# The last eighth of a split down projection: column half by column half, its sums merged into an early reloaded residual

## The chip, the cores and the metric

One Trainium2 chip, one of its cores. The metric is the device time of one execution in microseconds (us). The kernel before takes 873.03 us (median of 3 runs, 872.73 to 873.03).

## The reference

Two request groups of 256 tokens (512 rows, model width 1024) go through one encoder layer. Three attention branches are gated, summed and projected, a residual is added, and then comes the part at issue:

```python
h2 = rms_norm(x, norm2_g)
x = x + jnp.square(jax.nn.relu(h2 @ w_up)) @ w_down     # 1024 -> 4096 -> 1024
...
return rms_norm(x, final_norm_g)                        # over the whole row of 1024
```

All of it is float32.

## The kernel before

A float32 product is made of three passes on TensorE: each operand is split into a high part (a copy by ScalarE, in a rounded type) and a low part (original minus high, by VectorE), and `mm3` (L193) issues high x high, high x low, low x high. Splitting a weight chunk of 128x1024 is one ScalarE and one VectorE instruction, which write `w` tiles; the chunk arrives from memory by a transfer on SP's queue into one of two `raw` buffers (`chunk`, L163). A third chunk's transfer waits until the low part of the first is made.

The work is a list of units (`unit`, `run`, L178). `run` fetches the chunks of the units to come, as many ahead as `ahead[0]` says (3 in this stretch), and calls the units in turn. VectorE, ScalarE and TensorE keep the order in which the code issues (`InOrder`); SP's and POOL's queues are ordered by the framework's scheduler. `later` holds closures (evacuations, sums) that `flush` runs behind the next unit's matmuls or ahead of them; `lows` holds low parts that `lower` issues.

The MLP runs in 8 rounds (`NC`, L1045). Round c makes 512 of the 4096 hidden columns (`up`, in halves of 12 products each, `put_up` squares them) and, interleaved with these, seven products of the down projection of round c-1, in a scheme with fewer products than the plain one (Winograd's): `form` makes sums of hidden tiles, `parts` makes weight sums in `blk` tiles (4 per round, 8 buffers, `load_blocks` L900), `product` multiplies, and `add_to` adds the result to eight accumulators `acc` of 128x512, named V, 11, 12, 21 and G, two token tiles each. So a round is 15 x 12 products.

The last round's own hidden columns have nothing to interleave with: their down projection is done plainly, from `LAST` (four split hidden tiles of 128x512, the fourth made last) and four weight chunks 11, 12, 21, 22. There are 4 token tiles t of 128 rows and 2 column halves hh of 512, each of these 8 pieces needs 12 products. Before, `last_down(t)` does both halves of one t, `combine(t)` (L998) adds V to the accumulators and the sums to the residual tile `xt[t]`, and `finish` (L1023) adds the piece from PSUM, squares it on ScalarE for the final norm, and multiplies by the final gain `gf`. `final` (L1029) makes 1/rms on VectorE and POOL, scales the two halves on ScalarE and VectorE and writes them out. The residual (unscaled, stored in memory as `x1d` in round 0) and `gf` are fetched by `fetch_x1` (L987) behind the last round:

```python
    unit(fetch_x1)
    kept = []
    unit(lambda *w: (kept.extend(w), last_down(0, *w)), *[(block(NC - 1, n),) for n in ("11", "12", "21", "22")])
    for t in range(1, NT):
        unit(lambda t=t: last_down(t, *kept))
```

Of the kernel before, what the change touches and what calls it, by code (L numbers as in the profile page):

```python
# [10 lines left out]
F32 = mybir.dt.float32  # L11
F32R = mybir.dt.float32r
AF = mybir.ActivationFunctionType
ALU = mybir.AluOpType
AX = mybir.AxisListType

P = 128
# [3 lines left out]
NT = T // P  # L21
# [56 lines left out]
def encoder_kernel(ctx: ExitStack, tc: tile.TileContext, a: dict, out: bass.AP):  # L78
    nc = tc.nc
    V, A, E = (InOrder(tc, e) for e in (nc.vector, nc.scalar, nc.tensor))  # L80
    G, SP = nc.gpsimd, nc.sync

    sb = ctx.enter_context(tc.tile_pool(name="sb", bufs=1))
# [8 lines left out]
    def nm(s):  # L92
        cnt[0] += 1
        return f"{s}{cnt[0]}"
# [4 lines left out]
    def h2(s="h", dt=F32):  # L99
        return sb.tile([P, T], dt, tag="h2", name=nm(s), bufs=20)  # L100

    def bank(s="ps"):
        return ps.tile([P, 512], F32, tag="ps", name=nm(s))
# [36 lines left out]
    p = bank("warm")  # L140
# [6 lines left out]
    def unit(fn, *srcs):  # L147
        units.append((fn, srcs))
# [20 lines left out]
    ahead = [1]  # L169
# [3 lines left out]
    def lower(keep=0):  # L173
        for fn in lows[:len(lows) - keep]:
            fn()
        del lows[:len(lows) - keep]
# [16 lines left out]
    def mm3(o, wh, wl, xh, xl, first, last, more=False):  # L193

        E.matmul(o, wh, xh, start=first, stop=False, skip_group_check=more)
        E.matmul(o, wh, xl, start=False, stop=False, skip_group_check=more)
        E.matmul(o, wl, xh, start=False, stop=last, skip_group_check=more)
# [73 lines left out]
    later = []  # L271
# [395 lines left out]
    def flush(n=2):  # L667
        for fn in later[:n]:
            fn()
        del later[:n]  # L670
# [164 lines left out]
    NC = 8  # L835
# [10 lines left out]
    def block_tile():  # L846
        return at[0].tile([P, 1024], F32, tag="blk", name=nm("blk"), bufs=8)

    def turn_x1(t, hh):

        b = bank("tp")
        for i in range(4):
            E.transpose(b[:, i * P:(i + 1) * P], X1[4 * hh + i][:, t * P:(t + 1) * P], ident)
        x = h2("xt")
        A.activation(x, b, AF.Copy)
        A.activation(h2("junk"), b, AF.Square, accum_out=ss[:, t, hh:hh + 1])
        A.dma_start(x1d[t, :, hh * 512:(hh + 1) * 512], x)
# [11 lines left out]
    def up(w, ff, half):  # L869

        if half == 0:
            up_bank[ff] = w, bank()
        w, p = up_bank[ff]
        for k in range(4 * half, 4 * half + 4):
            c = slice(k * P, (k + 1) * P)
            mm3(p, w[0][:, c], w[1][:, c], H[k][:, 0], H[k][:, 1], k == 0, k == KD - 1)
        flush(9)
        if half:
            later.append(lambda: put_up(ff, p))
# [14 lines left out]
    LAST = []  # L894

    def block(c, n):
        k, h = ((0, 0), (0, 1), (1, 0), (1, 1))[("11", "12", "21", "22").index(n)]
        return a["w_dn"][c // 2, h, 2 * (c % 2) + k]

    def load_blocks(c):  # L900

        if c in blocks:
            return
        t = {n: block_tile() for n in "T2BC"}
        for n, b in (("T", "11"), ("2", "21"), ("C", "12"), ("B", "22")):
            SP.dma_start(t[n], block(c, b))
        G.dma_start(t["C"], block(c, "22"), accum_op=ALU.add)
        blocks[c] = t
# [20 lines left out]
    def form(c, name):  # L929

        lo, hi = UP[c, 0], UP[c, 1]
        A11, A21, A12, A22 = lo[:, :, :S], lo[:, :, S:], hi[:, :, :S], hi[:, :, S:]

        def less(u, v):
            d = h2("f").rearrange("p (j t) -> p j t", j=2)
            V.tensor_tensor(d, u, v, op=ALU.subtract)
            return d

        if name in ("P1", "P2", "Q4"):
            src = {"P1": A11, "P2": A12, "Q4": A22}[name]  # L940
        elif name == "Q5":
            src = forms[c, "S1"] = less(A21, A22)
        elif name == "Q6":
            src = forms[c, "S2"] = less(A11, forms.pop((c, "S1")))
        elif name == "P7":
            src = less(A11, A21)
        else:
            src = less(A12, forms.pop((c, "S2")))
        x = s4("f")
        xh, xl = (x[:, i].rearrange("p (j t) -> p j t", j=2) for i in range(2))  # L950
        A.activation(xh, src, AF.Copy)
        lows.append(lambda: V.tensor_tensor(xl, src, f(xh), op=ALU.subtract))
        forms[c, name] = x

    acc, banks = {}, {}
# [26 lines left out]
        later.append(lambda: [add_to(to, i, ps_[i], ALU.add if sign > 0 else ALU.subtract) for i in range(2)])  # L982


    xt, gf = {}, []

    def fetch_x1():  # L987
        for t in range(NT):
            xt[t] = sb.tile([P, 2, 512], F32, tag="s4", name=nm("xt"), bufs=21)
            SP.dma_start(xt[t], x1d[t].rearrange("p (h n) -> p h n", h=2))  # L990
        g = sb.tile([P, 2, 512], F32, tag="s4", name=nm("gf"), bufs=21)
        SP.dma_start(g, bass.AP(tensor=a["gf"].tensor, offset=a["gf"].offset, ap=[[0, P], [T, 2], [1, T]]))
        gf.append(g)

    def scaled(y, t, src):
        V.scalar_tensor_tensor(y, src, rr[:, t:t + 1], y, op0=ALU.mult, op1=ALU.add)

    def combine(t):  # L998
        i = t % 2
        for hh, k in enumerate(("11", "12") if t < 2 else ("21", "G")):  # L1000
            if k != "11":
                V.tensor_tensor(acc[k, i], acc[k, i], acc["V", i], op=ALU.subtract if k == "21" else ALU.add)
            scaled(xt[t][:, hh], t, acc[k, i])

    def last_down(t, *ws):
        c = slice(t * P, (t + 1) * P)
        flush(9)
        lower()
        later.append(lambda: combine(t))
        for hh in range(2):  # L1010
            cols = ((0, 256), (256, 512)) if t == NT - 1 and hh else ((0, 512),)
            for part, (n0, n1) in enumerate(cols):
                p = bank()[:, :n1 - n0]
                for k in range(4):
                    x, w = LAST[k], ws[2 * (k // 2) + hh]
                    n = slice((k % 2) * 512 + n0, (k % 2) * 512 + n1)
                    mm3(p, x[:, 0, c], x[:, 1, c], w[0][:, n], w[1][:, n], k == 0, k == 3)
                later.append(lambda hh=hh, p=p, n0=n0, n1=n1, part=part: finish(t, hh, p, n0, n1, hh + part))
        later.append(lambda: final(t, 2 + (t == NT - 1)))
        if t == NT - 1:  # L1020
            flush(9)

    def finish(t, hh, p, n0, n1, at_):  # L1023
        y = xt[t][:, hh, n0:n1]
        scaled(y, t, p)
        A.activation(h2("junk")[:, n0:n1], y, AF.Square, accum_out=fs[:, t, at_:at_ + 1])
        V.tensor_tensor(y, y, gf[0][:, hh, n0:n1], op=ALU.mult)

    def final(t, n):  # L1029
        r = fr[:, t:t + 1]  # L1030
        V.tensor_reduce(r, fs[:, t, :n], axis=AX.X, op=ALU.add)
        V.tensor_scalar(r, r, 1.0 / D, EPS, op0=ALU.mult, op1=ALU.add)
        G.tensor_tensor(r, r, mhalf[:, 0:1], op=ALU.pow)
        A.activation(xt[t][:, 0], xt[t][:, 0], AF.Copy, scale=r)
        V.tensor_scalar(xt[t][:, 1], xt[t][:, 1], r, None, op0=ALU.mult)
        for hh in range(2):
            (A, SP)[hh].dma_start(out[t * P:(t + 1) * P, hh * 512:(hh + 1) * 512], xt[t][:, hh])

    unit(mlp_pool)
    ORDER = ("P1", "P2", "Q5", "Q6", "P7", "Q3", "Q4")  # L1040

    def make(c, n):
        unit(lambda: form(c, ORDER[n]))

    for c in range(NC):  # L1045
        for h in range(8):
            ff, half = 4 * c + h // 2, h % 2
            unit(lambda *w, ff=ff, half=half: up(w[0] if w else None, ff, half), *([(a["w_up"][ff],)] if half == 0 else []))
            if c == 0:
                unit(lambda h=h: turn_x1(h % 4, h // 4))  # L1050
            if h == 1 and c < NC - 1:
                unit(lambda c=c: load_blocks(c))
            if c and h < 7:
                for n in ((1, 2) if h == 0 else (h + 2,)):
                    if n < 7:
                        make(c - 1, n)
                unit(lambda w, c=c - 1, n=ORDER[h]: product(w, c, n), (parts(c - 1, PRODUCTS[ORDER[h]][0]),))
        if c == 0:
            unit(inv_ms)
            unit(lambda: ahead.__setitem__(0, 3))  # L1060
        if c < NC - 1:
            make(c, 0)
    unit(fetch_x1)
    kept = []
    unit(lambda *w: (kept.extend(w), last_down(0, *w)), *[(block(NC - 1, n),) for n in ("11", "12", "21", "22")])
    for t in range(1, NT):
        unit(lambda t=t: last_down(t, *kept))
    run()


# [72 lines left out]
```

## Time and profile before

| what | value |
|---|---|
| median of 3 runs | 873.03 us |
| the profiled execution's own time | 873.93 us |
| its span | 872.2 us |
| busy: TensorE / VectorE / ScalarE / POOL | 844.6 / 465.7 / 397.3 / 215.6 us |
| share of the chain that ended last: TensorE / VectorE / ScalarE / DMA | 77% / 9% / 6% / 3% |
| granted TensorE clock, mean | 0.988 |

Times in the profile run from the start of the span. An instruction's idle time stands in brackets with what ended it. PE is TensorE, DVE VectorE, ACT ScalarE, SPq the issue of transfers on SP's queue. Since most operations go through one recording helper, they all show line 72; tiles tell them apart. A matmul's end is modelled, so the distance between starts is the measure. Two VectorE instructions that don't depend on each other overlap by about 0.08 us in the rows.

### The profile page before, as it was taken

The page shows a single profiled execution, that of the slowest core. Times are in us where ns is not written, and L with a number is a line of the kernel's source. Part 1 is how long each engine was busy: PE and PEld are TensorE (multiplying, and loading weights), DVE is VectorE, ACT ScalarE, POOL GpSimd, SP SyncE. Part 2 cuts the span into 40 slices and gives each one's busy share as a digit, 9 for nine tenths or more (in the row PEclk, how much of TensorE's full clock was granted, in tenths as well). Part 3 has the DMA queues.
Part 4 walks back from the last instruction along what each step waited for, and adds up shares of the span by engine and source line. Part 5 has one row for each costly group of instructions (what it writes and reads, how often), then busy time and mean ns, then how long its engine had stood idle before and what let it go on. Part 6 is the DMA issues. An engine that isn't in the chain of part 4 may idle for free.

```text
span 872.2 us, 10787 instructions
## 1 busy us (share of the span) xinstructions
PE 844.6 (97%) x4080; PEld 702.1 (81%) x4080; DVE 465.7 (53%) x741; ACT 397.3 (46%) x690; POOL 215.6 (25%) x161
## 2 busy tenths in 40 slices
PE   9999999999999999999999999999999999999972
PEld 7778998888888888888887888888888888888762
DVE  6595445455543213333336443566675858576655
ACT  6364555565554333232224356555353535444432
POOL 2315455557556552112212000010000100000000
PEclk9999999999999999999999999999999999999986
DMA  8242223233331138222323445465655657434501
GB/s 292 104 136 85 85 73 105 78 96 104 98 98 66 57 143 285 96 79 91 121 78 114 146 159 155 121 175 140 168 143 147 163 128 197 85 104 96 192 27 73
DMA packets 47468, 106.87 MB, mean 123 GB/s; under 512 B 19358, under 2 KB 19604, under 8 KB 47416
## 3 DMA queue, kind: packets, MB, share of 16 engines
q1 hardware_dynamic: 39992, 85.69, 29.8%
q0 software_dynamic: 4256, 14.73, 9.5%
q10 hardware_dynamic: 3168, 5.77, 1.9%
q8 instruction: 32, 0.52, 0.3%
q14 instruction: 20, 0.16, 0.1%
HBM read 101.93 MB, written 4.24 MB: 122 GB/s over the span
## 4 chain that ended last, share of the span: by engine, by line
PE 77%; DVE 9%; ACT 6%; issue 3%; DMA 3%; POOL 1%; SPq 0%; POOLq 0%; DVEq 0%; ACTq 0%
PE ps L72 70%; DVE w L72 3%; PE sc L72 3%; PE o L72 2%; ACT w L72 2%; PE tp L72 2%; DMA mr<-in_memT 1%; DVE xt L72 1%; DVE f L72 1%; DMA raw<-in_w_dn 1%; DVE acc L72 1%; DMA raw<-in_w_mem 1%; ACT f L72 1%; ACT sp L72 1%; ACT r L72 1%
## 5 line engine op out<-in xcount | busy, mean ns | idle before, releaser
L72 PE MATMUL ps<-x,w 128*128 128x512 f32 x1080 | 252.5, 391 | 0.0
L72 PEld LDWEIGHTS ps<-x,w 128*128 128x128 f32 x1080 | 200.8, 188 | 41.5
L72 PE MATMUL ps<-h,w 128*128 128x512 f32 x768 | 184.5, 390 | 0.0
L72 PE MATMUL ps<-w,f 128*128 128x512 f32 (+1 forms) x696 | 167.1, 391 | 6.5 <-ACT f L72 4.9
L72 PEld LDWEIGHTS ps<-h,w 128*128 128x128 f32 x768 | 143.6, 188 | 29.6
L72 DVE TENSOR_TENSOR w<-raw,w 128x1024 fp32r<-128x1024 f32 (+1 forms) x79 | 96.3, 1223 | 122.9 <-ACT w L72 122.7
L72 PEld LDWEIGHTS ps<-w,f 128*128 128x128 f32 x696 | 130.2, 190 | 36.6 <-ACT f L72 5.3
L72 ACT ACTIVATE w<-raw 128x1024 fp32r<-128x1024 f32 (+2 forms) x116 | 119.8, 1036 | 31.1 <-DMA raw<-in_w_dn 10.4
L161 POOL TENSOR_TENSOR w<-raw,w 128x1024 fp32r<-128x1024 f32 (+1 forms) x37 | 87.4, 2361 | 118.1 <-ACT w L72 95.3
L72 DVE TENSOR_TENSOR w<-blk,w 128x1024 fp32r<-128x1024 f32 x49 | 59.4, 1222 | 48.0 <-ACT w L72 48.0
L921 POOL DMA_DIRECT2D blk<-in_w_dn x21 | 18.1, 864 | 239.8 <-DVE w L72 239.8
L72 DVE TENSOR_TENSOR acc<-acc,ps 128x512 f32<-128x512 f32 x88 | 56.6, 680 | 3.1 <-PE ps L72 3.1
L72 ACT ACTIVATE w<-blk 128x1024 fp32r<-128x1024 f32 x49 | 50.7, 1047 | 15.1 <-DMA blk<-in_w_dn 15.1
L72 ACT ACTIVATE sp<-sp,st 128x256 f32<-128x256 f32 (+1 forms) x48 | 25.8, 538 | 57.8 <-DVE st L72 57.8
L72 ACT ACTIVATE f<-f 128x512 fp32r<-128x512 f32 x28 | 17.7, 632 | 74.3 <-DVE f L72 74.3
L72 ACT ACTIVATE g<-ps 128x512 f32<-128x512 f32 x16 | 9.6, 598 | 88.4 <-PE ps L72 88.4
L72 PE MATMUL ps<-mg,w 128*128 128x512 f32 x192 | 44.3, 390 | 1.5 <-ACT mg L72 0.9
L72 DVE TENSOR_TENSOR sum<-o,lo 64x256 f32<-64x256 f32 x24 | 10.0, 417 | 66.4 <-ACT lo L72 66.2
L72 PEld LDWEIGHTS ps<-mg,w 128*128 128x128 f32 x192 | 36.0, 188 | 9.6 <-ACT mg L72 1.3
L72 ACT ACTIVATE r<-ps 128x512 f32<-128x512 f32 x32 | 18.9, 591 | 46.4 <-PE ps L72 46.4
L72 PE MATMUL ps<-w,x 128*128 128x384 f32 (+1 forms) x192 | 39.9, 362 | 0.0
L469 POOL TENSOR_TENSOR sp<-sp,st 128x512 f32<-128x512 f32 (+1 forms) x32 | 36.7, 1147 | 6.2 <-DVE st L72 3.1
(147 smaller groups left out, 951.3 us busy)
## 6 DMA issues: line engine op xcount, KB each, us to landing
raw<-in_w_up SPq DMA_DIRECT2D x32, 512.0 KB, 4.2
blk<-in_w_dn SPq DMA_DIRECT2D x28, 512.0 KB, 6.8
blk<-in_w_dn POOLq DMA_DIRECT2D x28, 512.0 KB, 5.5
raw<-in_w_g SPq DMA_DIRECT2D x24, 512.0 KB, 3.2
raw<-in_w_b SPq DMA_DIRECT2D x12, 512.0 KB, 3.3
raw<-in_w_bam SPq DMA_DIRECT2D x8, 512.0 KB, 3.3
raw<-in_w_o SPq DMA_DIRECT2D x8, 512.0 KB, 3.2
raw<-in_w_mem SPq DMA_DIRECT2D x7, 512.0 KB, 3.2
```

Source lines behind the costliest of these rows:

```text
L72: return self.tc.keep_in_program_order(method(*args, **kw))
L161: sub[0].tensor_tensor(lo[:, c], raw[:, c], f(hi[:, c]), op=ALU.subtract)
L469: G.tensor_tensor(s[:, :, :w], s[:, :, :w], st[:, 6:8].unsqueeze(2).to_broadcast([P, 2, w]), op=ALU.mult)
L921: G.dma_start(src, block(c, n[1:]), accum_op=ALU.add)
```

## The change

The residual is fetched in the last round, behind its second half-up (`h == 1`, where the other rounds load their blocks), into the `blk` tiles that this round would not use; `gf` with it. The sums of the accumulators are put among the last round's units (22 at h = 5, 12 at h = 6, 11 at h = 7, 21 behind the first two pieces). The last eighth is taken column half by column half: chunks 11 and 21 first and all four t with hh = 0, then chunks 12 and 22 and hh = 1. The first unit takes t = 0 and 1 together, with the products of the first three hidden tiles of both ahead of those of the fourth. From h = 6 on, 2 chunks are fetched ahead instead of 3.

```diff
     def fetch_x1():
         for t in range(NT):
-            xt[t] = sb.tile([P, 2, 512], F32, tag="s4", name=nm("xt"), bufs=21)
+            xt[t] = block_tile().rearrange("p (h n) -> p h n", h=2)
             SP.dma_start(xt[t], x1d[t].rearrange("p (h n) -> p h n", h=2))
...
-    def combine(t):
-        i = t % 2
-        for hh, k in enumerate(("11", "12") if t < 2 else ("21", "G")):
-            if k != "11":
-                V.tensor_tensor(acc[k, i], acc[k, i], acc["V", i], op=ALU.subtract if k == "21" else ALU.add)
-            scaled(xt[t][:, hh], t, acc[k, i])
...
+    def combine(n):
+        k = "G" if n == "22" else n
+        for i in range(2):
+            t = 2 * (n[0] == "2") + i
+            if n != "11":
+                V.tensor_tensor(acc[k, i], acc[k, i], acc["V", i], op=ALU.subtract if n == "21" else ALU.add)
+            scaled(xt[t][:, int(n[1]) - 1], t, acc[k, i])
+
+    def down(p, t, hh, ks, n0=0, n1=512):
         c = slice(t * P, (t + 1) * P)
+        for k in ks:
+            x, w = LAST[k], kept[k // 2, hh]
+            n = slice((k % 2) * 512 + n0, (k % 2) * 512 + n1)
+            mm3(p, x[:, 0, c], x[:, 1, c], w[0][:, n], w[1][:, n], k == 0, k == 3)
+
+    def last_down(hh, ts, n0=0, n1=512, part=0):
         flush(9)
         lower()
-        later.append(lambda: combine(t))
-        for hh in range(2):
-            cols = ((0, 256), (256, 512)) if t == NT - 1 and hh else ((0, 512),)
...
+        ps_ = {t: bank()[:, :n1 - n0] for t in ts}
+        for ks in ((0, 1, 2), (3,)) if len(ts) > 1 else (range(4),):
+            for t in ts:
+                down(ps_[t], t, hh, ks, n0, n1)
+        for t in ts:
+            later.append(lambda t=t, p=ps_[t]: finish(t, hh, p, n0, n1, hh + part))
+            if hh and n1 == 512:
+                later.append(lambda t=t: final(t, 2 + part))
...
+    SUMMED = {5: "22", 6: "12", 7: "11"}
...
-            if h == 1 and c < NC - 1:
-                unit(lambda c=c: load_blocks(c))
+            if h == 1:
+                unit(lambda c=c: load_blocks(c) if c < NC - 1 else fetch_x1())
+            if c == NC - 1 and h == 6:
+                unit(lambda: ahead.__setitem__(0, 2))
+            if c == NC - 1 and h in SUMMED:
+                unit(lambda n=SUMMED[h]: later.append(lambda: combine(n)))
...
-    unit(fetch_x1)
-    kept = []
-    unit(lambda *w: (kept.extend(w), last_down(0, *w)), *[(block(NC - 1, n),) for n in ("11", "12", "21", "22")])
-    for t in range(1, NT):
-        unit(lambda t=t: last_down(t, *kept))
+    unit(lambda *w: (kept.update({(0, 0): w[0], (1, 0): w[1]}), last_down(0, (0, 1))),
+         *[(block(NC - 1, n),) for n in ("11", "21")])
+    unit(lambda: later.append(lambda: combine("21")))
+    for t in (2, 3):
+        unit(lambda t=t: last_down(0, (t,)))
+    unit(lambda *w: (kept.update({(0, 1): w[0], (1, 1): w[1]}), last_down(1, (0,))),
+         *[(block(NC - 1, n),) for n in ("12", "22")])
+    for t in (1, 2):
+        unit(lambda t=t: last_down(1, (t,)))
+    for part in range(2):
+        unit(lambda n=part: last_down(1, (3,), 256 * n, 256 * n + 256, n))
+    unit(lambda: flush(9))
```

What this moves on the queues. First SP, from the last-but-two transfer of `w_up` to the last weight chunk. `raw` are weight chunks; the residual is `xt` before and, since it lies in the blocks' buffers, `blk` in the change. Before:

```order
L165 DMA raw_6597<-in_w_up 128x1024
L165 DMA raw_6684<-in_w_up 128x1024
L165 DMA raw_6743<-in_w_dn 128x1024
L165 DMA raw_6765<-in_w_dn 128x1024
L990 DMA xt_6803<-x1d 128x1024
L990 DMA xt_6805<-x1d 128x1024
L165 DMA raw_6783<-in_w_dn 128x1024
L990 DMA xt_6807<-x1d 128x1024
L990 DMA xt_6809<-x1d 128x1024
L992 DMA gf_6811<-in_gf 128x1024
L165 DMA raw_6813<-in_w_dn 128x1024
```

And in the change:

```order
L990 DMA blk_6555<-x1d 128x1024
L990 DMA blk_6557<-x1d 128x1024
L165 DMA raw_6506<-in_w_up 128x1024
L990 DMA blk_6559<-x1d 128x1024
L165 DMA raw_6607<-in_w_up 128x1024
L165 DMA raw_6694<-in_w_up 128x1024
L992 DMA gf_6561<-in_gf 128x1024
L165 DMA raw_6757<-in_w_dn 128x1024
L165 DMA raw_6779<-in_w_dn 128x1024
L165 DMA raw_6849<-in_w_dn 128x1024
L165 DMA raw_6855<-in_w_dn 128x1024
```

The five residual and gain transfers no longer stand among the four weight chunks. (The first residual tile, not shown, stands two `w_up` chunks further up.)

Second ScalarE, from the third hidden tile's high part (`f`) to the fourth's; `r` and `u` are the fourth's relu and square, `w` are high parts of weights. Before:

```order
L72 ACTIVATE f_6741<-u_6737 128x512
L72 ACTIVATE w_6744<-raw_6743 128x1024
L72 ACTIVATE w_6766<-raw_6765 128x1024
L72 ACTIVATE w_6784<-raw_6783 128x1024
L72 ACTIVATE w_6814<-raw_6813 128x1024
L72 ACTIVATE r_6819<-ps_6750 128x512
L72 ACTIVATE u_6737<-r_6819 128x512
L72 ACTIVATE f_6822<-u_6737 128x512
```

And in the change:

```order
L72 ACTIVATE f_6751<-u_6747 128x512
L72 ACTIVATE w_6758<-raw_6757 128x1024
L72 ACTIVATE w_6780<-raw_6779 128x1024
L72 ACTIVATE r_6815<-ps_6764 128x512
L72 ACTIVATE u_6747<-r_6815 128x512
L72 ACTIVATE f_6818<-u_6747 128x512
L72 ACTIVATE w_6850<-raw_6849 128x1024
L72 ACTIVATE w_6856<-raw_6855 128x1024
```

The fourth hidden tile stood behind all four weight chunks and now stands behind two.

Third VectorE, from the last sums of the product Q3 on (`acc<-acc,ps`); `w` and `f` are low parts, `xt` or `blk` the residual. Before:

```order
L72 TENSOR_TENSOR acc_4762<-acc_4762,ps_6700 128x512
L72 TENSOR_TENSOR w_6745<-raw_6743,w_6744 128x1024
L72 TENSOR_TENSOR f_6741<-u_6737,f_6741 128x512
L72 TENSOR_TENSOR acc_4881<-acc_4881,ps_6608 128x512
L72 TENSOR_TENSOR acc_4883<-acc_4883,ps_6615 128x512
L72 TENSOR_TENSOR w_6767<-raw_6765,w_6766 128x1024
L72 TENSOR_TENSOR w_6785<-raw_6783,w_6784 128x1024
L72 TENSOR_TENSOR acc_4918<-acc_4918,ps_6693 128x512
L72 TENSOR_TENSOR acc_4920<-acc_4920,ps_6700 128x512
L72 TENSOR_TENSOR w_6815<-raw_6813,w_6814 128x1024
L72 TENSOR_TENSOR f_6822<-u_6737,f_6822 128x512
L72 SCALAR_TENSOR_TENSOR xt_6803<-acc_4715,rr,xt_6803 128x512
```

And in the change:

```order
L72 TENSOR_TENSOR acc_4762<-acc_4762,ps_6710 128x512
L72 TENSOR_TENSOR acc_4760<-acc_4760,acc_4663 128x512
L72 SCALAR_TENSOR_TENSOR blk_6557<-acc_4760,rr,blk_6557 128x512
L72 TENSOR_TENSOR acc_4762<-acc_4762,acc_4665 128x512
L72 SCALAR_TENSOR_TENSOR blk_6559<-acc_4762,rr,blk_6559 128x512
L72 TENSOR_TENSOR w_6759<-raw_6757,w_6758 128x1024
L72 TENSOR_TENSOR f_6751<-u_6747,f_6751 128x512
L72 TENSOR_TENSOR acc_4881<-acc_4881,ps_6618 128x512
L72 TENSOR_TENSOR acc_4883<-acc_4883,ps_6625 128x512
L72 TENSOR_TENSOR w_6781<-raw_6779,w_6780 128x1024
L72 TENSOR_TENSOR acc_4881<-acc_4881,acc_4663 128x512
L72 SCALAR_TENSOR_TENSOR blk_6553<-acc_4881,rr,blk_6553 128x512
```

Four instructions of the sums (22) now stand ahead of the first weight chunk's low part; behind these rows follow the rest of 12, two sums from PSUM, the two of 11, the fourth hidden tile's low part and the low parts of the other two chunks. The queue has the same 737 instructions as before.

## Rows read from the trace of the kernel before

**Rows 1.** The page's head: the span, and each engine's busy time, share of the span and instructions.

```profile
span 872.2 us, 10787 instructions
...
PE 844.6 (97%) x4080; PEld 702.1 (81%) x4080; DVE 465.7 (53%) x741; ACT 397.3 (46%) x690; POOL 215.6 (25%) x161
```

**Rows 2.** Busy time of each engine in stretches of the end (first column the stretch, then its length; PEclk is the clock granted to TensorE as a share of 2.4 GHz).

```profile
820.00:830.00 10.00, 7.85 (x34) 5.86 (x32) 4.18 (x6) 1.06 (x1) 0.00 (x0) 1.00 0.73 262
...
840.00:850.00 10.00, 10.00 (x46) 8.29 (x45) 6.35 (x14) 2.90 (x7) 0.97 (x2) 1.00 0.14 54
...
856.00:873.00 17.00, 0.00 (x0) 0.00 (x0) 8.06 (x18) 3.91 (x10) 1.10 (x2) 0.58 0.16 62
```

**Rows 3.** TensorE's instructions in order of time, from the last half-up (`h,w`) on: start, length, what, how many; in brackets the idle time before and what ended it. The rows with `w,f` are `last_down` (99 in the last one, 24 of them of half the width).

```profile
822.65 2.88 PE L72 MATMUL ps<-h,w 128*128 128x512 f32 x12
825.37 1.75 PE L72 MATMUL ps<-w,f 128*128 128x512 f32 x7
827.43 0.73 PE L72 MATMUL ps<-w,f 128*128 128x512 f32 x2 [0.31 <-DVE w L72]
833.04 22.66 PE L72 MATMUL ps<-w,f 128*128 128x512 f32 x99 [4.88 <-ACT f L72]
```

**Rows 4.** ScalarE's instructions in order of time: the high parts of weight chunks 2, 3 and 4 and of the fourth hidden tile.

```profile
817.93 1.06 ACT L72 ACTIVATE w<-raw 128x1024 fp32r<-128x1024 f32 x1 [0.36 <-DMA raw<-in_w_dn]
825.05 1.06 ACT L72 ACTIVATE w<-raw 128x1024 fp32r<-128x1024 f32 x1 [6.07 <-DMA raw<-in_w_dn]
830.13 1.06 ACT L72 ACTIVATE w<-raw 128x1024 fp32r<-128x1024 f32 x1 [4.01 <-DMA raw<-in_w_dn]
...
832.36 0.63 ACT L72 ACTIVATE f<-u 128x512 fp32r<-128x512 f32 x1
```

**Rows 5.** SP's queue in order of time: issues of transfers (a merged row ends with its last issue).

```profile
802.05 12.62 SPq L165 DMA_DIRECT2D raw<-in_w_dn  x2
814.73 0.90 SPq L990 DMA_DIRECT2D xt<-x1d  x2
818.86 0.33 SPq L165 DMA_DIRECT2D raw<-in_w_dn  x1
819.23 0.91 SPq L990 DMA_DIRECT2D xt<-x1d  x2
...
821.79 0.33 SPq L165 DMA_DIRECT2D raw<-in_w_dn  x1
```

**Rows 6.** Issues by tile over the whole run: how many, KB each, median us from issue to landing.

```profile
blk<-in_w_dn SPq DMA_DIRECT2D x28, 512.0 KB, 6.8
...
raw<-in_w_dn SPq DMA_DIRECT2D x4, 512.0 KB, 5.8
xt<-x1d SPq DMA_DIRECT2D x4, 512.0 KB, 5.7
```

**Rows 7.** All chunk transfers into `raw` from 700 us on: shortest, median and longest time to landing.

```profile
DMA to landing us min/median/max: 3.1/4.2/8.2
```

**Rows 8.** VectorE's instructions in order of time: the end of the last round, then the sums (850.59) and the two pieces of t = 2, its `final` (857.66), the start of t = 3 (859.06), the last half piece and the last `final`.

```profile
815.97 1.27 DVE L72 TENSOR_TENSOR acc<-acc,ps 128x512 f32<-128x512 f32 x2
817.60 1.23 DVE L72 TENSOR_TENSOR w<-raw,w 128x1024 fp32r<-128x1024 f32 x1 [0.35 <-ACT w L72]
...
826.15 1.23 DVE L72 TENSOR_TENSOR w<-raw,w 128x1024 fp32r<-128x1024 f32 x1 [4.39 <-ACT w L72]
...
831.22 1.23 DVE L72 TENSOR_TENSOR w<-raw,w 128x1024 fp32r<-128x1024 f32 x1 [2.65 <-ACT w L72]
833.02 0.69 DVE L72 TENSOR_TENSOR f<-u,f 128x512 fp32r<-128x512 f32 x1 [0.58 <-ACT f L72]
...
839.26 0.75 DVE L72 SCALAR_TENSOR_TENSOR xt<-ps,rr,xt 128x512 f32<-128x512 f32 x1 [1.35 <-PE ps L72]
...
850.59 0.69 DVE L72 TENSOR_TENSOR acc<-acc,acc 128x512 f32<-128x512 f32 x1
...
853.37 0.74 DVE L72 SCALAR_TENSOR_TENSOR xt<-ps,rr,xt 128x512 f32<-128x512 f32 x1
...
857.66 0.15 DVE L72 TENSOR_REDUCE fr<-fs 128x1 f32<-128x2 f32 x1
...
859.06 0.69 DVE L72 TENSOR_TENSOR acc<-acc,acc 128x512 f32<-128x512 f32 x1
...
865.37 0.48 DVE L72 SCALAR_TENSOR_TENSOR xt<-ps,rr,xt 128x256 f32<-128x256 f32 x1
...
866.77 0.15 DVE L72 TENSOR_REDUCE fr<-fs 128x1 f32<-128x3 f32 x1
```

**Rows 9.** Busy time of each engine and granted clock in a short stretch, columns as in rows 2.

```profile
833.00:835.00 2.00, 1.96 (x5) 1.53 (x6) 1.96 (x3) 0.00 (x0) 0.00 (x0) 0.50 0.00 0
```

**Rows 10.** SP's queue one round earlier, where the blocks of round 6 are loaded at the same place of the program.

```profile
723.40 6.15 SPq L906 DMA_DIRECT2D blk<-in_w_dn  x2
731.56 0.33 SPq L165 DMA_DIRECT2D raw<-in_w_up  x1
733.29 0.33 SPq L906 DMA_DIRECT2D blk<-in_w_dn  x1
```

**Rows 11.** ScalarE's use of the chunk that SP issued at 731.56.

```profile
744.27 1.04 ACT L72 ACTIVATE w<-raw 128x1024 fp32r<-128x1024 f32 x1
```

**Rows 12.** The stretch in which round 6's blocks and chunks are used, columns as in rows 2.

```profile
740.00:780.00 40.00, 39.83 (x176) 32.71 (x175) 27.35 (x35) 19.34 (x26) 2.14 (x3) 1.00 0.41 101
```

More of the change, by code (lines that the diff above doesn't have):

```diff
@@ L982, in product @@
         later.append(lambda: [add_to(to, i, ps_[i], ALU.add if sign > 0 else ALU.subtract) for i in range(2)])
-    xt, gf = {}, []
+    xt, gf, kept = {}, [], {}
     def fetch_x1():
         for t in range(NT):
-            xt[t] = sb.tile([P, 2, 512], F32, tag="s4", name=nm("xt"), bufs=21)
+            xt[t] = block_tile().rearrange("p (h n) -> p h n", h=2)
             SP.dma_start(xt[t], x1d[t].rearrange("p (h n) -> p h n", h=2))
@@ L996, in scaled @@
         V.scalar_tensor_tensor(y, src, rr[:, t:t + 1], y, op0=ALU.mult, op1=ALU.add)
-    def combine(t):
-        i = t % 2
-        for hh, k in enumerate(("11", "12") if t < 2 else ("21", "G")):
-            if k != "11":
-                V.tensor_tensor(acc[k, i], acc[k, i], acc["V", i], op=ALU.subtract if k == "21" else ALU.add)
-            scaled(xt[t][:, hh], t, acc[k, i])
-    def last_down(t, *ws):
-        c = slice(t * P, (t + 1) * P)
+    def combine(n):
[6 more added lines that the diff above has]
+    def down(p, t, hh, ks, n0=0, n1=512):
+        c = slice(t * P, (t + 1) * P)
+        for k in ks:
[3 more added lines that the diff above has]
+    def last_down(hh, ts, n0=0, n1=512, part=0):
         flush(9)
         lower()
-        later.append(lambda: combine(t))
-        for hh in range(2):
-            cols = ((0, 256), (256, 512)) if t == NT - 1 and hh else ((0, 512),)
[L1012 to L1021, printed above, removed]
+        ps_ = {t: bank()[:, :n1 - n0] for t in ts}
[6 more added lines that the diff above has]
+                later.append(lambda t=t: final(t, 2 + part))
     def finish(t, hh, p, n0, n1, at_):
```

## The prediction

> **What bounds the kernel now.** I read the page's head first: TensorE is busy 97% of the span [rows 1], so over the whole kernel nothing else counts. But the change touches the last 55 us only, and there the table by stretches says something else [rows 2]. From 820 to 830 TensorE is busy 7.85 of 10 us; behind 856 it does nothing for 16 us, while VectorE is still at work. So I read the engines' queues in order of time there.
>
> TensorE starts `last_down(0)` at 825.37, does the nine products of the first three hidden tiles, and stops for 4.88 us at 828.16 for the fourth hidden tile's high part [rows 3]. That tile stands on ScalarE behind weight chunks 3 and 4, which wait 6.07 and 4.01 us for their transfers [rows 4]. Those stand on SP's queue between and behind four residual tiles and the gain, 512 KB each, and need up to 8.2 us to land where 3.1 is the shortest [rows 5, 7]. After the stop TensorE's granted clock is 0.50, 1.2 GHz [rows 9]: the 87 products that are left (in units of 512 columns) take 22.7 us, at 0.227 each (twelve from 822.65 to 825.37) they would take 19.7 [rows 3].
>
> TensorE is done at 855.70 [rows 3]. The end at 872.2 is VectorE's: it goes through t = 2 in 859.06 - 850.59 = 8.5 us, where TensorE gives a t every 24 x 0.227 = 5.4 us, so it falls behind. From 833 on it waits for TensorE once, 1.35 us at 839.26; its other gaps are the short waits for ScalarE's square and POOL's power inside `finish` and `final`. Ahead of 833 it has gaps of 0.35, 4.39, 2.65 and 0.58 us, all behind ScalarE's copies of late chunks [rows 8]. **VectorE's queue from 816 us on, with these gaps, sets the end.**
>
> **The change, part by part.** VectorE gets no instruction more or less; from 817.2 on it does the same set in another order. So the end moves by the gaps that go, less those that come.
>
> *Gaps that go.* 0.35 + 4.39 + 2.65 + 0.58 + 1.35 = 9.32 us [rows 8]. Where no gap is, neighbours overlap by 0.08 (two sums of 0.68 take 1.27 at 815.97 [rows 8]): 5 x 0.08 = 0.4 more. Together 9.7 us.
>
> *Gaps that could come.* I walk the new queue with durations less 0.08: low part of a chunk 1.15, of a hidden tile 0.6, two sums from PSUM 1.2, four instructions of a `combine` 2.78 (850.59 to 853.37), a piece 2.14 (half of 853.37 to 857.66), `final` 1.40 (857.66 to 859.06), a half piece 1.40 (865.37 to 866.77), and 872.2 - 866.77 = 5.43 from the last reduction to the end [rows 8].
> - 817.2: sums 22, to 820.0. They need the residual of t = 2 and 3 (below).
> - 820.0: low part of chunk 1, hidden tile 3, two sums, to 822.9. Chunk 1's high part is done before 817.93.
> - 822.9: chunk 2, whose high part ends at 819.0 [rows 4]; sums 12, two sums from the last product (TensorE gave it before 822.65 + 0.4), two of 11: to 829.4.
> - 829.4: low part of hidden tile 4. On ScalarE it now follows chunk 2, so it is made as soon as the last half-up is done at 825.6, in 1.9 us as from 831.1 to 833.0 [rows 3, 4]: 827.5. No gap. Done at 830.1. TensorE needs it for its 21st product, at 825.37 + 20 x 0.227 = 829.9: a stop of 0.2 us, at most 0.5, in place of 4.88; too short to price beyond that.
> - 830.0 and 831.15: chunks 3 and 4. Their transfers are issued as the low parts of 1 and 2 end, 821.2 and 824.1. Landing takes 3.1 to 8.2 us [rows 7]; I take 3.5, since nothing else is on the queues then: 824.7 and 827.6, high parts by 828.6 and 829.6, in time. With 8.2 chunk 4's high part would end at 833.4 and VectorE would wait 2.3 us: the upper bound.
> - 832.3: first `finish`; TensorE gave that piece at 830.3. Four pieces and sums 21: 832.3 + 4 x 2.14 + 2.78 = 843.6. Three pieces with `final`, 3 x 3.54: 854.3. Two half pieces: 857.1. End: 857.1 + 5.43 = **862.5**, 9.7 below 872.2, as the gaps gave.
> - TensorE does 96 products from 825.37 and ends at 847.4, 7 us ahead of what VectorE does with its last piece; its saved stop and clock are worth nothing by themselves, they only take the 1.35 away.
>
> *The reload.* Its transfers come into round 7 where rounds 1 to 6 load their blocks. One round earlier those were issued by 723.4, 729.2 and 733.3 [rows 10], and a round is 180 x 0.227 = 40.8 us: so by 774.1 now, and at 6.8 us (5.7 for xt before) [rows 6] landed by 781, 36 us ahead of sums 22. Ahead of `w_up` on SP's queue they cost what the blocks cost: the chunk issued at 731.56 between them was used at 744.27 without a wait, a cover of 12.7 us against 8.2 at worst [rows 7, 10, 11], and TensorE is busy 39.83 of 40 us there [rows 12]. I cost this at nothing; without that cover each microsecond of lateness would stop TensorE. The gain's transfer, behind the last `w_up` chunk, has no neighbour and is free. Fetching 2 ahead instead of 3 moves chunks 3 and 4 behind the hidden tile, counted above.
>
> Sum: -9.7 us. The profiled execution's own time is 873.93, 0.9 above the median, so 864.2 for one like it and 873.03 - 9.7 = **863.3** against the median. 0.2% is 1.75 us, about what a measurement can tell.
>
> **Rivals.**
> 1. *TensorE sets the end.* If VectorE had caught up, the end would be TensorE's end plus what follows the last half piece: 847.4 + (872.2 - 865.37) = 854.2, 18 us less, 855.0 [rows 3, 8]. For it speaks the 97%; against it the 8.5 us per t before, of which the 2.78 of sums go elsewhere, but not off VectorE. The Trainium skill points this way (Perfetto Trace Analysis, Optimization Strategies, under DMA performance): keep the matmul engine busy, and speed up whichever engine it waits for. The rows agree on the stop and its cause, and differ on what it is worth here. 0.03.
> 2. *The second pair of chunks lands late.* The cost is up to 2.3 us on VectorE, with the order's small waits up to 866.0. For it: two of four such transfers took 6 and 8 us; against: both shared the queues with the residual. 0.14.
> 3. *The reload lands late, and VectorE stands at sums 22,* with the low parts of chunk 1 and 2 and hidden tile 3 and 4 queued behind; TensorE waits for those. Place: the second instruction of sums 22 at 817.9. Price: 1 us for each, with no cover from 817.9 on. Were the reload as late as in the kernel before (issued by 820.1 [rows 5] plus 5.7: 825.8), 7.9 of the 9.7 would go back, 871.2; landing later than 827.6 makes the kernel **slower**, at 832 by 4.4 us, 877.4. That needs one residual transfer held on SP by a block's buffer that is free only at the round's end. Against it: 36 us of margin. Slower 0.03, a gain that is only part or nothing 0.04.
>
> **How the numbers follow.** The forecast has 0.76, with a range of its own of 862.2 to 864.6 (0.2 to 0.5 for TensorE's stop, half a microsecond for overlaps over some 60 instructions, 0.3 for the runs). 861.8 to 866.2 takes in rival 2 and leaves out 1 and 3, 0.10. Faster by over 0.2%: the forecast, rivals 1 and 2, and half of the 0.04: 0.95. Same 0.02, slower 0.03.
>
> **What the profile would show.** Right: the four `x1d` issues before 780; VectorE without a gap for ScalarE or TensorE from 817 to the first piece at about 832, other than the short ones in `finish` and `final`; TensorE's stop near 829.9 under 0.5 us and its clock at 1.00 until about 847; a last reduction near 857. Wrong: a gap on VectorE in front of a residual sum or of chunk 4's low part, idle TensorE ahead of 825, or VectorE waiting for TensorE in the last pieces.

## The result, and the profile after

The changed kernel takes **866.79 us** (median of 4 runs: 866.86, 866.90, 866.72, 864.78), the kernel before 873.03 beside it (4 runs, 872.73 to 873.09): a ratio of 0.9924 [0.9907, 0.9941], 6.2 us less. The forecast was 863.3, and the range ended at 866.2. Measured again with more runs (below) it is 865.41 against 874.01, 0.9904 [0.9890, 0.9919], 8.6 us less. The profiled execution's own time is 866.86, its span 865.1. One of the ten executions of the kernel before that stand beside some of the experiments below (median 873.68) took 1273.97 us at a mean granted clock of 0.62; it is slow, and no ratio uses it.

The stretches, columns as in [rows 2]:

```profile
820.00:830.00 10.00, 10.00 (x46) 8.28 (x45) 9.86 (x15) 3.06 (x5) 0.00 (x0) 1.00 0.32 105
830.00:840.00 10.00, 9.87 (x44) 7.86 (x43) 8.38 (x12) 3.15 (x6) 0.00 (x0) 1.00 0.01 2
840.00:850.00 10.00, 10.00 (x57) 8.71 (x55) 6.87 (x13) 2.90 (x7) 0.57 (x1) 1.00 0.00 0
```

From 820 to 830 TensorE was busy 7.85 us and VectorE 4.18 [rows 2]; now it is 10.00 and 9.86, and the clock is granted in full up to 850, where it was 0.50 behind the stop [rows 9]. TensorE's rows, to be held against [rows 3]:

```profile
822.23 2.88 PE L72 MATMUL ps<-w,f 128*128 128x512 f32 x12
824.95 2.88 PE L72 MATMUL ps<-h,w 128*128 128x512 f32 x12
827.67 22.50 PE L72 MATMUL ps<-w,f 128*128 128x512 f32 x108
```

The stop of 4.88 us is gone; what is left of it hides in the 0.13 us that TensorE is idle from 830 to 840. But the last half-up begins at 824.95 and not at 822.65: **2.30 us are lost before the changed stretch begins.** VectorE, to be held against [rows 8]:

```profile
818.42 1.28 DVE L72 TENSOR_TENSOR acc<-acc,ps 128x512 f32<-128x512 f32 x2
819.61 0.69 DVE L72 TENSOR_TENSOR acc<-acc,acc 128x512 f32<-128x512 f32 x1
820.33 0.75 DVE L72 SCALAR_TENSOR_TENSOR blk<-acc,rr,blk 128x512 f32<-128x512 f32 x1
...
822.39 1.22 DVE L72 TENSOR_TENSOR w<-raw,w 128x1024 fp32r<-128x1024 f32 x1
...
831.76 0.68 DVE L72 TENSOR_TENSOR f<-u,f 128x512 fp32r<-128x512 f32 x1
832.36 2.35 DVE L72 TENSOR_TENSOR w<-raw,w 128x1024 fp32r<-128x1024 f32 x2
834.63 0.74 DVE L72 SCALAR_TENSOR_TENSOR blk<-ps,rr,blk 128x512 f32<-128x512 f32 x1
836.17 0.69 DVE L72 TENSOR_TENSOR blk<-blk,gf 128x512 f32<-128x512 f32 x1 [0.79 <-ACT junk L72]
...
859.34 0.42 DVE L72 TENSOR_TENSOR blk<-blk,gf 128x256 f32<-128x256 f32 x1 [0.57 <-ACT junk L72]
859.69 0.15 DVE L72 TENSOR_REDUCE fr<-fs 128x1 f32<-128x3 f32 x1
```

No gap stands between 818.42 and the first piece at 834.63; behind it VectorE waits only inside `finish` and `final`, never for TensorE. From the last sums of Q3 to the last reduction it takes 859.69 - 818.42 = 41.27 us. SP's queue, to be held against [rows 5]:

```profile
741.49 0.33 SPq L990 DMA_DIRECT2D blk<-x1d  x1
...
767.49 6.15 SPq L990 DMA_DIRECT2D blk<-x1d  x2
...
777.39 0.32 SPq L990 DMA_DIRECT2D blk<-x1d  x1
...
804.48 22.41 SPq L165 DMA_DIRECT2D raw<-in_w_dn  x4
```

The last residual tile is issued at 777.39, 43 us ahead of the first sum that needs the residual (820.33). The landing times, to be held against [rows 6]:

```profile
blk<-x1d SPq DMA_DIRECT2D x4, 512.0 KB, 6.0
raw<-in_w_dn SPq DMA_DIRECT2D x4, 512.0 KB, 4.0
```

The weight chunks land in 4.0 us instead of 5.8 with the residual gone from among them.

Where the 2.30 us went is found by going back along TensorE's rows to where the two traces part: the rms norm ahead of the first products.

```profile
39.52 2.54 PE L72 MATMUL ps<-ones,sq 128*128 128x1 f32 x14 [0.17 <-DVE sq L72]
41.92 5.37 PE L72 MATMUL ps<-w,m 128*128 128x512 f32 x12
47.13 1.02 PE L72 MATMUL ps<-xd,ones 128*128 128x512 f32 x2
```

In the kernel before:

```profile
39.66 1.72 PE L72 MATMUL ps<-ones,sq 128*128 128x1 f32 x14 [0.17 <-DVE sq L72]
41.25 3.01 PE L72 MATMUL ps<-w,m 128*128 128x512 f32 x12
44.79 1.13 PE L72 MATMUL ps<-xd,ones 128*128 128x512 f32 x2 [0.53 <-DVE xd L72]
```

The twelve wide products take 5.37 us instead of 3.01, and the next ones start 2.34 us later. In stretches of 5 us the clock was 1.00 from 40 to 50 us in the profile of before. First its line, then the two lines of after:

```profile
40.00:45.00 5.00, 4.47 (x26) 3.61 (x26) 2.83 (x6) 0.00 (x0) 3.32 (x5) 1.00 0.32 107
...
40.00:45.00 5.00, 5.00 (x19) 4.38 (x19) 2.91 (x6) 0.00 (x0) 3.47 (x6) 0.52 0.34 108
45.00:50.00 5.00, 5.00 (x17) 3.69 (x16) 1.92 (x3) 0.99 (x2) 1.45 (x3) 0.80 0.46 137
```

0.52 is about the lower level, 1.2 GHz. No line there is touched by the change. So two questions: does the tail do what was forecast, and does this fall of the clock belong to the change? For the first I use one measure in every profile, the **tail**: from the start of the last half-up (the last `ps<-h,w` row of TensorE) to the end of the span. It was 872.2 - 822.65 = 49.55, was forecast at 862.5 - 822.65 = 39.85, and is 865.1 - 824.95 = 40.15.

### The profile page after: what moved, and what is told of

Its sections match the earlier page's. It is cut to its first block, busy times and chain, and to the rows that moved or that the text cites. A ratio compares the mean times of both kernels' runs of the same rounds, so it can differ in the third digit from the quotient of the medians.

```text
span 865.1 us, 10788 instructions
## 1 busy us (share of the span) xinstructions
PE 845.0 (98%) x4080; PEld 703.2 (81%) x4080; DVE 464.4 (54%) x741; ACT 397.8 (46%) x690; POOL 215.8 (25%) x161
## 4 chain that ended last, share of the span: by engine, by line
PE 76%; DVE 12%; ACT 6%; issue 3%; DMA 2%; POOL 0%; SPq 0%; POOLq 0%; DVEq 0%; ACTq 0%
PE ps L72 69%; DVE w L72 3%; PE sc L72 3%; PE o L72 2%; ACT w L72 2%; PE tp L72 2%; DVE blk L72 2%; DVE acc L72 2%; DMA mr<-in_memT 1%; DVE f L72 1%; DMA raw<-in_w_mem 1%; ACT sp L72 1%; ACT junk L72 1%; DVE sp L72 1%; ACT f L72 1%
## 5 line engine op out<-in xcount | busy, mean ns | idle before, releaser
L72 PE MATMUL ps<-w,f 128*128 128x512 f32 (+1 forms) x696 | 164.4, 387 | 1.4 <-DVE acc L72 1.0
```

The costliest lines, as they stand in the source:

```text
L72: return self.tc.keep_in_program_order(method(*args, **kw))
```

## Experiments

**The changed kernel once more, in more runs.** No edit.

> The changed kernel once more, as it is. The trace of the changed kernel has its end as worked out (the last reduction 41.3 us behind the last sums of Q3, 41.1 were forecast), but TensorE reaches the last half-up 2.3 us later than before: its granted clock is 0.50 from 40.4 to 47 us, in the stretch of one-column products, which no line of the change touches; one of its four times is 864.78 with a mean clock of 0.991, the others 866.7 to 866.9 at 0.989 to 0.990. Theory (chance): the early half clock comes and goes with the execution, in either kernel: times fall into two groups, near 864.8 and near 866.8 here, and the kernel before may show the like 2 us above 873.0. Rival (the change brings it): the kernel before never has it (all at 872.7 to 873.1), the changed one in most runs, at 866.8.

Measured: 865.41 (6 runs, 863.98 to 867.42) against 874.01 (23 runs, 871.58 to 875.76), 0.9904 [0.9890, 0.9919]. In its profile the tail is 865.6 - 825.55 = 40.05, and the granted clock is 0.56 from 40 to 45 us. The two shortest executions, 863.98 and 864.07, have spans of 862.2 and 862.3 and a mean clock of 0.994, where the profiled one has 0.989; the forecast span was 862.5. That fits executions without the early fall, but they have no profile that would show it. So the tail repeats to 0.1 us (a variant below, with the table products moved, has 866.8 - 826.66 = 40.1 too), and single executions of either kernel differ by 3 to 4 us.

**The kernel before, profiled a second and a third time.** No edit.

> The kernel before once more, for a second profile of it. Theory (an execution's gaps vary with how its transfers land, and the early half clock comes and goes in this kernel too): from the last half-up to the end 47.5 to 49.6 us, VectorE's gaps not the same as in the first profile; with or without a half clock at 40 to 47 us. Rival (the first profile is what this kernel always does): 49.5 us, the same gaps within 0.2 us, no early half clock.

> The kernel before a third time, for its profile. Theory: from the last half-up to the end between 47.5 and 49.6 us again, not the same as in the two others (49.6 and 48.3), with the gaps of VectorE that differ following the landing of the third and fourth weight chunk.

Measured: own times 874.91 and 873.41, spans 873.1 and 871.6. The last half-up starts at 824.82 and 823.49, so the tails are 48.3 and 48.1: the 49.55 on which the forecast rested is the longest of the three (mean 48.65). Two variants of this kernel, further below, change nothing near the end and add two tails: 876.4 - 827.28 = 49.1 and 872.1 - 824.30 = 47.8. The mean of all five is 48.6. From 40 to 45 us the clock is 0.53 and 0.74: **the kernel before has the early fall too.** The stretch in the second profile:

```profile
40.00:45.00 5.00, 5.00 (x19) 4.32 (x19) 2.92 (x6) 0.00 (x0) 3.54 (x6) 0.53 0.30 108
```

VectorE's gaps ahead of the fourth hidden tile's low part in the second profile:

```profile
826.68 1.23 DVE L72 TENSOR_TENSOR w<-raw,w 128x1024 fp32r<-128x1024 f32 x1 [2.75 <-ACT w L72]
832.45 1.22 DVE L72 TENSOR_TENSOR w<-raw,w 128x1024 fp32r<-128x1024 f32 x1 [3.35 <-ACT w L72]
834.26 0.69 DVE L72 TENSOR_TENSOR f<-u,f 128x512 fp32r<-128x512 f32 x1 [0.58 <-ACT f L72]
```

The same gaps as in [rows 8], but 2.75 and 3.35 for 4.39 and 2.65 (2.91 and 2.83 in the third): they follow the landings of chunks 3 and 4, which differ from execution to execution. From issue to ScalarE's copy it is 6.2 us for chunk 3 and 8.3 for chunk 4 in the first profile, 4.6 and 7.4 in the second, 4.7 and 7.0 in the third.

**The reload alone.** The kernel before with its old order of pieces and sums; only `fetch_x1` moves.

```diff
-            xt[t] = sb.tile([P, 2, 512], F32, tag="s4", name=nm("xt"), bufs=21)
+            xt[t] = block_tile().rearrange("p (h n) -> p h n", h=2)
...
-            if h == 1 and c < NC - 1:
-                unit(lambda c=c: load_blocks(c))
+            if h == 1:
+                unit(lambda c=c: load_blocks(c) if c < NC - 1 else fetch_x1())
...
-    unit(fetch_x1)
```

> The kernel before with one part of the change: residual and gain are fetched in the last round into the free block buffers; order of the pieces, sums and weight chunks as before. Theory (VectorE's gaps ahead of 833 come from weight chunks that share the queues with the reload): chunks 3 and 4 land in about 3.5 us instead of 6.2 and 8.3, VectorE's gaps ahead of its first piece shrink from 8.0 to about 3 us, TensorE's stop from 4.9 to under 1.5, and from the start of the last half-up to the end of the span it takes about 43 us, against 49.6 in the profiled execution before and 40.1 in the changed kernel. Rival (the order of the pieces is what counts, the transfers' company does not): the chunks take 6 to 8 us as before, 48 to 49 us.

Measured: 868.99 (4 runs) against 873.68, 0.9947 [0.9933, 0.9961]; tail 868.3 - 825.12 = 43.2. VectorE:

```profile
820.07 1.23 DVE L72 TENSOR_TENSOR w<-raw,w 128x1024 fp32r<-128x1024 f32 x1 [0.29 <-ACT w L72]
...
825.74 1.23 DVE L72 TENSOR_TENSOR w<-raw,w 128x1024 fp32r<-128x1024 f32 x1 [1.51 <-ACT w L72]
...
828.81 1.23 DVE L72 TENSOR_TENSOR w<-raw,w 128x1024 fp32r<-128x1024 f32 x1 [0.65 <-ACT w L72]
830.62 0.69 DVE L72 TENSOR_TENSOR f<-u,f 128x512 fp32r<-128x512 f32 x1 [0.59 <-ACT f L72]
```

The gaps shrink, since chunks 3 and 4 now land in 3.4 us each, but they stay. The residual's place on SP's queue is worth 48.65 - 43.18 = 5.5 us by the tail, of 8.5 for the whole change; by the medians it is 4.7 of 8.6.

**Without the new order of pieces.** The changed kernel with the reload and the early sums, but t by t as before and 3 chunks ahead.

```diff
-            if c == NC - 1 and h == 6:
-                unit(lambda: ahead.__setitem__(0, 2))
...
-    unit(lambda *w: (kept.update({(0, 0): w[0], (1, 0): w[1]}), last_down(0, (0, 1))),
-         *[(block(NC - 1, n),) for n in ("11", "21")])
+    unit(lambda *w: (kept.update({(0, 0): w[0], (0, 1): w[1], (1, 0): w[2], (1, 1): w[3]}), last_down(0, (0,))),
+         *[(block(NC - 1, n),) for n in ("11", "12", "21", "22")])
+    unit(lambda: last_down(1, (0,)))
...
     for t in (1, 2):
-        unit(lambda t=t: last_down(1, (t,)))
+        for hh in range(2):
+            unit(lambda t=t, hh=hh: last_down(hh, (t,)))
+    unit(lambda: last_down(0, (3,)))
```

> The changed kernel without its order of pieces: reload and sums early as changed, but all four weight chunks fetched ahead of the first piece and both column halves of a token tile in a row, as before. Theory: the fourth hidden tile stands behind chunks 3 and 4 on ScalarE again, so TensorE stops 3 to 4.5 us near 828 and runs at 0.50 clock after it; VectorE, ahead of TensorE then, waits for pieces: 42 to 44 us from the last half-up to the end instead of 40.1. Rival (TensorE's stop is worth nothing, since VectorE sets the end): 40.1 to 40.5 us.

Measured: 868.38 (4 runs) against 873.68, 0.9937 [0.9923, 0.9951]; tail 866.7 - 822.73 = 44.0. TensorE:

```profile
828.38 0.73 PE L72 MATMUL ps<-w,f 128*128 128x512 f32 x2 [1.18 <-DVE w L72]
830.71 0.74 PE L72 MATMUL ps<-w,f 128*128 128x512 f32 x2 [1.59 <-ACT f L72]
832.64 22.52 PE L72 MATMUL ps<-w,f 128*128 128x512 f32 x97 [1.20 <-DVE f L72]
```

And the two waits of VectorE for it:

```profile
833.48 0.75 DVE L72 SCALAR_TENSOR_TENSOR blk<-ps,rr,blk 128x512 f32<-128x512 f32 x1 [0.89 <-PE ps L72]
...
838.60 0.75 DVE L72 SCALAR_TENSOR_TENSOR blk<-ps,rr,blk 128x512 f32<-128x512 f32 x1 [2.89 <-PE ps L72]
```

With sums done early, VectorE has no gap before 832.6, but TensorE stops for 1.18 + 1.59 + 1.20 us, its clock is 0.66 from 830 to 840, and VectorE then waits 3.78 us for pieces. The tail is 3.9 us longer than the changed kernel's. TensorE's stop, hidden behind VectorE's gaps before, sets the end once those are gone. The order of the pieces and the fetching of 2 chunks ahead go together here; no run parts them.

**Without the early sums.** The changed kernel with its order of pieces; sums 22, 12 and 11 stand where they are first needed (`last_down` gets a parameter `sums`).

```diff
+        for n in sums:
+            later.append(lambda n=n: combine(n))
...
-            if c == NC - 1 and h in SUMMED:
-                unit(lambda n=SUMMED[h]: later.append(lambda: combine(n)))
...
```

> The changed kernel with reload and order of pieces as changed, but the sums 22, 12 and 11 at the place where they are first needed, behind the last products instead of among them. Theory (the sums are free only where VectorE would stand still, and the order of pieces makes it stand still): VectorE waits about 1.2 us for the last product of the seven, 3.4 us for the fourth hidden tile and under 1 us for chunks, which the sums 22 and 12 (2 x 2.78 us) filled; so 45.5 us from the last half-up to the end instead of 40.1, more than the reload alone (43.2). Rival (the order alone gives most of it, as the transfers no longer wait): 41 us or less.

Measured: 871.89 (10 runs) against 874.03, 0.9973 [0.9961, 0.9985]; tail 870.7 - 825.29 = 45.4. VectorE's largest gap:

```profile
830.17 0.69 DVE L72 TENSOR_TENSOR f<-u,f 128x512 fp32r<-128x512 f32 x1 [3.99 <-ACT f L72]
```

TensorE has no stop here, and VectorE waits 0.42 us in all for chunks, yet 45.4 - 40.1 = 5.3 of the 8.5 us are gone: from 826 to 830 VectorE has nothing it may do, and does the sums later, when pieces wait.

**The changed kernel with the gain's multiply put one place back.** In `finish` VectorE waits 0.79 us for ScalarE's square before it multiplies by the gain in place. Here the multiply (and `final`) is issued behind the next piece's first instruction.

```diff
-                later.append(lambda t=t: final(t, 2 + part))
+                later.append(lambda t=t: behind.append(lambda: final(t, 2 + part)))
...
-        V.tensor_tensor(y, y, gf[0][:, hh, n0:n1], op=ALU.mult)
+        due, behind[:] = list(behind), [lambda: V.tensor_tensor(y, y, gf[0][:, hh, n0:n1], op=ALU.mult)]
+        for fn in due:
+            fn()
...
```

> The changed kernel, with the multiplication by the final gain put behind the next piece's first instruction on VectorE, so that VectorE does not stand still 0.79 us for ScalarE's square in each piece. Nothing else differs, TensorE's end included. Theory (VectorE's queue sets the end, TensorE is 7 us ahead): a piece takes 1.3 instead of 2.14 us, 8 pieces and 2 halves give up to 7 us, until the end is TensorE's: 33 to 35 us from the last half-up to the end instead of 40.1, and 6 us less in time. Rival (TensorE or ScalarE sets the end): under 1 us.

Measured: **858.97** (5 runs, 858.49 to 860.60) against 873.68, 0.9829 [0.9816, 0.9843], the best version; tail 858.8 - 824.09 = 34.7. VectorE:

```profile
834.01 1.40 DVE L72 SCALAR_TENSOR_TENSOR blk<-ps,rr,blk 128x512 f32<-128x512 f32 x2
835.55 0.69 DVE L72 TENSOR_TENSOR blk<-blk,gf 128x512 f32<-128x512 f32 x1
...
843.99 0.75 DVE L72 SCALAR_TENSOR_TENSOR blk<-ps,rr,blk 128x512 f32<-128x512 f32 x1 [1.20 <-PE ps L72]
```

And the last of TensorE's rows:

```profile
831.88 17.67 PE L72 MATMUL ps<-w,f 128*128 128x512 f32 x88 [0.37 <-DVE f L72]
```

The 0.79-us waits are gone, and VectorE now catches up with TensorE and waits 1.20 us for a piece, though TensorE's own stop is only 0.37 us.

**The early fall of the clock: three tries at its cause.** The products of one column (`ps<-ones,sq`) stand behind four small ones for a bias table (`ps<-oh,tab`). The theory was that this run of small products lets the clock fall. First the changed kernel, then the kernel before, with the table products moved behind the next half; then the kernel before with them doubled.

```diff
-    unit(tables)
...
+    unit(tables)
```

> The changed kernel, with the bias tables' products (36 rows, 20 columns out) moved behind twelve full products, so that they no longer stand directly ahead of the one-column products. Theory (the clock falls because some 4 us of small products stand in a row): the granted clock stays at 1.00 from 30 us on, every run is at 862.5 to 864.8 and the spread of the times goes. Rival (the fall has to do with the change, or with what the first transfers do): the half clock stays somewhere between 35 and 50 us in most runs, 866 to 867.

> The kernel before with the same move of the bias tables. Theory: it had full clock there anyway, so it stays within 0.7 us of 873.0 (the move may take away TensorE's 0.53 us wait at 44.8); with e2 it gives the change's worth without the early clock, 8.3 to 9.7 us. Rival (the move itself is what speeds e2 up): 2 us less, 871.

```diff
-            E.matmul(p[0:20, :w], tab, o[0:36, :w], start=True, stop=True)
+            for _ in range(2):
+                E.matmul(p[0:20, :w], tab, o[0:36, :w], start=True, stop=True)
```

> The kernel before with the bias tables' products done twice: 1.7 us more of small products ahead of the one-column ones. Theory: that stretch, long enough, makes the clock fall in any kernel: 0.50 from about 40 us for some 6 us, 873.0 + 1.7 + 2.3 = 877.0. Rival (the change brings it): the clock stays at 1.00 and only the 1.7 us are added, 874.7 or less.

Measured: 868.38 and 875.81 with the tables moved, 3.0 us above the changed kernel and 1.8 above the one before (1.0022 [1.0010, 1.0033]); 875.18 with them doubled (1.0018 [1.0005, 1.0031]). Both times with the tables moved lie above everything that was forecast for them. In the first, a stretch shows that the fall is still there (in the second it is 0.56):

```profile
40.00:45.00 5.00, 5.00 (x19) 4.52 (x19) 1.76 (x4) 0.00 (x0) 1.03 (x1) 0.50 0.31 105
```

The theory fell: moving the table products does not keep the clock up, and it opens a gap of 1.56 us on TensorE that they had filled. Doubling them left a shorter fall (0.73 from 40 to 45 us) in the one profile. The forecasts were 4.0 us more by the theory and at most 1.7 by its rival, counted from 873.0; against the kernel before measured beside it, 874.01, it is 1.2 us more. That is the rival's size and speaks against a full fall in every execution, but since part of the fall is there, it does not settle what brings it.

## Why the prediction was wrong

**The mechanism held.** VectorE's queue from 816 us on sets the end, its gaps go, and nothing comes in their place. One account covers all these kernels: VectorE's waits for ScalarE's copies, for TensorE and for the squares, from the last sums of Q3 on, plus the 0.08 us of overlap that each costs, say how long the tail is.

| kernel | VectorE's waits that the changed kernel does not have, us | with 0.08 for each | tail above the changed kernel's 40.1 |
|---|---|---|---|
| before [rows 8] | 0.35 + 4.39 + 2.65 + 0.58 + 1.35 | 9.7 | 9.4 |
| before, second profile | 2.75 + 3.35 + 0.58 + 1.07 | 8.1 | 8.2 |
| before, third profile | 0.39 + 2.91 + 2.83 + 0.58 + 1.23 | 8.3 | 8.0 |
| before, tables moved | 0.27 + 2.13 + 4.38 + 0.58 + 1.49 | 9.3 | 9.0 |
| before, tables doubled | 0.18 + 3.20 + 2.84 + 0.58 + 0.62 | 7.8 | 7.7 |
| reload alone | 0.29 + 1.51 + 0.65 + 0.59 | 3.4 | 3.1 |
| without the new order | 0.89 + 2.89 | 3.9 | 3.9 |
| without the early sums | 0.16 + 0.50 + 3.99 + 0.26 | 5.2 | 5.3 |

Step by step:

- *The walk of the new queue: right.* From the sums at 815.97 to the last reduction it gave 857.1 - 815.97 = 41.1 us; measured 41.27. That VectorE's work is the same holds too: both traces count 741 of its instructions (not 737, as the section on the change has it). The tail was forecast at 39.85 and measured at 40.05 to 40.15.
- *TensorE's stop of 0.2, at most 0.5: right* (0.13 us idle from 830 to 840, clock 1.00 to 850).
- *The second pair of chunks in time, the reload 36 us ahead: right* (the chunks land in 4.0 us at the median; the last residual tile is issued 43 us ahead of its use and, at 6.0 us, there 37 us ahead). Rivals 2 and 3 did not come about.
- *Rival 1, TensorE sets the end: not for this change.* VectorE never waits for it. But the step "its saved stop and clock are worth nothing by themselves" held only under VectorE's old gaps: with these gone and the order left as it was, the stops, with the lower clock behind them, cost 3.9 us. The rule of the Trainium skill that was weighed there (Perfetto Trace Analysis, Optimization Strategies: keep the matmul engine busy) agrees with that run. The best version's gain has another source: there TensorE is done 9 us before the end (831.88 + 17.67 = 849.55 of 858.8), and 5.4 us come from VectorE's order alone.
- **The step that failed: the base, "873.03 - 9.7", with "0.3 for the runs".** It has two halves. First, 9.7 is the sum of one execution's gaps, and that execution's tail is the longest of three: the mean of the three is 48.65 (48.6 with the two variants), so the change is worth 48.65 - 40.1 = **8.5 us** and not 9.7; the medians of the second measurement say 8.6. The row that could have warned is [rows 7]: transfers of one kind landing in anything from 3.1 to 8.2 us, with gaps that hang on them, are no constant. Second, the clock's fall at 40 us is worth 2.3 us between the two profiles, far above 0.3. Both profiles of the changed kernel had it; of the three of before one had it in full, one in part, and the first, from which the forecast was made, not at all. No term of the sum allows for it.

The sum, put right, for the profiled execution: forecast 873.93 - 9.7 = 864.23; + 2.30 for the early fall, + 0.30 for the tail, + 0.03 around the span (866.86 - 865.1 against 873.93 - 872.2) = 866.86, its own time. Against the median the forecast took off another 0.9, which again is one execution's distance from its neighbours and no constant.

That most of the first measurement's changed runs, but not those of before, had the early fall would explain why it shows 6.2 us where the second shows 8.6: 8.5 - 2.3 = 6.2. For it speaks the mean clock: three of the four changed runs have 0.989 to 0.990, as the profiled one. This is argued and was not shown; the unprofiled runs give no stretches. What remains open is why the clock falls in one execution and not in the next.

The parts don't add up: by the tail the reload alone is worth 5.5 us, with the early sums but the old order 48.65 - 43.97 = 4.7, with the new order but late sums 3.2, all three 8.5. By the medians it is 4.7, 5.3, 2.1 and 8.6, so which of the first two is better stays open. Without gaps for chunks, VectorE waits either for pieces that TensorE gives late (old order) or at the fourth hidden tile with nothing else to do (late sums); each of the two edits takes away the wait that the other leaves.

## What to carry to other kernels

Where one engine's queue sets the end, its waits in order of time gave the length of the tail to 0.3 us here, but take them from two or three profiles of the kernel before if they hang on transfers, and split the time at an instruction ahead of the change so that what happens before it isn't counted. Work that depends on nothing late (here the sums of the accumulators) is worth most in the place where that engine waits anyway. When a gap is closed, look again at the engine that was not the bound: a stop that cost nothing may now set the end.

## What was not expected of the hardware

- TensorE's granted clock falls soon after 40 us, in a stretch of small products for a table, products of one column and twelve wide ones, though its rows leave hardly a gap (0.17 us in the changed kernel from 37.3 to 47.6). Of twelve profiles, of both kernels and variants of each, seven show 0.50 to 0.57 from 40 to 45 us, three 0.73 to 0.80, two 1.00 (the first of before and that without the new order). The last half-up starts at 822.65 and 822.73 in the last two, at 824.8 to 825.6 in the five with the full fall and the table products in place.
- A wait of VectorE for a square that ScalarE makes from its result is 0.79 us at 128x512 wherever it stands in the changed kernel's tail. It is the square and the read of its sum, which keep ScalarE from 835.41 to 836.14 for the first piece. Nine such waits (7 x 0.79 + 0.80 + 0.57 = 6.9 us) were in the changed kernel's tail; putting an independent instruction between took 40.1 - 34.7 = 5.4 us off the end, and about as much as the rest came back as new waits, 1.20 us for TensorE and 0.46 for the last square.
